# A third form tile, later stores of the gated blocks, and one pass of taps for the last column block

## The chip, the cores and the metric

The kernel runs on one core of one Trainium2 chip. The metric is the time of one execution on the device in microseconds (us). The engines go by their profile names: PE is TensorE, DVE is VectorE, ACT is ScalarE, POOL is GpSimd, and SP is SyncE, which here only issues DMA transfers. POOL issues transfers of its own, through another queue.

## The reference

A decoder layer for 256 tokens and 2048 features, in float32. The normalised input is projected once into ten parts. Two mixers use them: attention with 16 heads over low-rank latents, and a short causal convolution. Each passes a gate and a projection, and the two are merged by sigmoid gates.

```python
h = _rmsnorm(x, pre_norm_g)
(q_a, c_kv, k_rope, z_mla, c_in, b_gate, c_gate, z_conv,
 g_mla, g_conv) = jnp.split(h @ w_in, cuts, axis=-1)
q = _rmsnorm(q_a, q_a_norm_g) @ w_q_b        # 16 heads of 128 + 64 (rotary)
kv = _rmsnorm(c_kv, kv_a_norm_g) @ w_kv_b    # 16 heads of 128 + 128
attn = _causal_mla_attention(q_nope, q_rope, k_nope, k_rope, v)
y_mla = (attn * jax.nn.silu(z_mla)) @ w_o_mla
u = c_gate * c_in
u_pad = jnp.pad(u, ((0, 0), (CONV_K - 1, 0), (0, 0)))
conv = sum(conv_w[k] * u_pad[:, k:k + s] for k in range(CONV_K))   # CONV_K = 3
y_conv = (b_gate * conv * jax.nn.silu(z_conv)) @ w_o_conv
merged = jax.nn.sigmoid(g_mla) * y_mla + jax.nn.sigmoid(g_conv) * y_conv
x = x + _rmsnorm(merged @ w_out, post_norm_g)
```

## The kernel before

**Splitting.** Every float32 operand of a matmul is split into a rounded part and a rest. ACT copies the rounded part (`whi`), DVE subtracts it to get the rest (`wlo`), and PE adds three products: hi by hi, hi by lo, lo by hi. Weights come in units of 128 x 2048 numbers (1 MB) into three `raw` buffers. SP loads a unit once the DVE instruction that made the rest of the unit three before it is done. Four k-blocks of weights against both token tiles are 24 matmuls of width 512, called a unit here.

**Stage one: latents.** The products for `qa`, `ckv` and `kr`, and the tables `cos_t`, `sin_t` of the rotation.

**Stage two: the loop over 16 heads** (line 996). Each head h makes, beside its attention, one quarter of the work on a column block of 512 convolution channels: `channels(h, i)` for i = 0 to 3 is one weight unit each, and head 4j + n makes c_gate, c_in, b_gate, z_conv (n = 0 to 3) of block j. The banks `cv` are evacuated by ACT or DVE (lines 811 to 820) before the next head needs them. Between the units stand scores, softmax, `turn` and `values` of neighbouring heads. Two side jobs are cut into steps by generators:

- `make_forms` (line 871) prepares seven sums of quarters of the normalised input for the Winograd products of stage three: "11", "22", "12", "5", "6", "7" and "3", in four chunks, so 28 pieces. One step is taken at three places in each of the heads 0 to 13. In a step, `part` (line 900) takes a tile `form` from a ring of two, ACT writes its hi half (line 902), DVE its lo half (line 904 or 906). SP is told to store it to `far_form` (line 909) in the step after. Four small tiles, `u, w, f7, f3`, hold sums (line 897).
- `taps(j, t)` (line 831) makes the convolution of block j and token tile t. It brings two copies of u shifted by one and two tokens through POOL transfers into `mv1`, `mv2` and two weight rows into `cw`; in a second step it multiplies and adds them and fetches the third weight row; in a third step it finishes in `cv_f` (all products at line 853). Each token tile is a run of its own; for block 3, tile 1 is begun at the end of head 13 and tile 0 in head 14, and tile 0 ends in head 15. `channels_join` then multiplies the gate in and stores the block, turned, through POOL to `far_cv`.

**Stage three: the square products.** A list `seq` of units, in four sets (s0 to s3, "set one" to "set four" here), interleaves two kinds. `branch_block` units multiply the mixers' outputs by w_o (banks `sq`). `paired` units make two gate blocks at a time by a Winograd scheme over the forms (banks `sX`, `sZ`, `sY`; tiles `b`), with some sums made by adding POOL transfers (line 1256). When a gate tile `sa` to `sd` and its product meet, set one and two call `weigh` (line 1216): multiply, and store to `kept` one unit later on SP (line 1148). Set three and four call `merge` (line 1230): multiply, add the block fetched again into a tile `y` (POOL, line 1151), transpose on DVE (line 358), and store to `far_m` one unit later by four SP transfers (line 366). `later(n, fn)` puts fn off by n units. A store that is issued on SP waits there for its tile, and whatever is behind it in SP's queue waits too. `turned_unit` (line 964) reloads `far_at`, `far_cv` and `far_m` for the next products.

**Stage four: out.** 16 weight units against the four merged blocks `m_both`; blocks 0 and 1 are needed at once, block 2 at the fifth unit, block 3 at the seventh. Then the last norm.

The order of PE is the program's. On ACT and DVE a scheduler sets it from its estimates, but for the instructions marked by `keep_in_program_order`; the orders of SP and POOL are the program's too.

Of the kernel before, what the change touches and what calls it, by code (L numbers as in the profile page):

```python
# [82 lines left out]
def tile_layer(ctx: ExitStack, tc: tile.TileContext, xw, w0, xb, x, pos, pvec, post_g, wc, wz, wcv, wkr, wqk, wqr, wv, cwr, wsq, xf, out):  # L83
# [211 lines left out]
    cos_t = const.tile([P, S], F32, name="cos_t")  # L295
    sin_t = const.tile([P, S], F32, name="sin_t")
# [34 lines left out]
    ckv = lp.tile([P, KR, 2 * S], F32R, name="ckv")  # L331
    kr = bp.tile([P, 2, S], F32R, name="kr")
# [498 lines left out]
    def taps(j, t):  # L831

        u, parts = cv_t[:, j, t, :], []

        def bring(dst, src):

            tc.keep_in_program_order(nc.gpsimd.dma_start(out=dst, in_=src))

        for d in (1, 2):
            m = temp(f"mv{d}", (P, 512), bufs=1, tag=f"mv{d}x")  # L840
            if t:
                bring(m[:d, :], cv_t[P - d :, j, 0, :])
            else:
                tc.keep_in_program_order(nc.gpsimd.memset(m[:d, :], 0.0))
            bring(m[d:, :], u[: P - d, :])
            parts.append(m[:, :])
        def tap(d):
            cw = temp("cw", (P, 512), bufs=2)
            bring(cw[:, :], cwr[2 - d : 3 - d, 512 * j : 512 * (j + 1)].to_broadcast([P, 512]))
            return cw  # L850

        def join(dst, a, b, op):
            tc.keep_in_program_order(nc.vector.tensor_tensor(dst, a, b, op=op))
# [17 lines left out]
    def make_forms():  # L871
# [3 lines left out]
        sums_4 = [early_pool.tile([P, kq, P], F32, name=f"form_sum{i}") for i in range(4)]  # L875
        for c in range(KH // kq):
# [17 lines left out]
            u, w, f7, f3 = (f[:, :, :] for f in sums_4)  # L894
# [4 lines left out]
            def part(n, src, sign=1.0):  # L899
                f = early_pool.tile([P, kq, 2, P], F32R, name=f"form{n}_{c}", tag="form", bufs=2)  # L900
                hi, lo = f[:, :, 0, :], f[:, :, 1, :]
                nc.scalar.activation(hi, src, AF.Copy, scale=sign)
                if sign == 1.0:
                    nc.vector.tensor_tensor(lo, src, hi.bitcast(F32), op=ALU.subtract)
# [11 lines left out]
                ("5", u, 1.0, (w, u, a11, ALU.add)), ("6", w, -1.0, (f7, a11, a21, ALU.subtract)),  # L916
                ("7", f7, 1.0, (f3, w, a12, ALU.subtract)), ("3", f3, 1.0, None),
# [78 lines left out]
    for h in range(H):  # L996
        v, at = divmod(h, HV)

        if h == H - 2:
            estack.close()  # L1000
            lstack.close()
            fleft = main.enter_context(tc.tile_pool(name="fleft", bufs=1, reuse_waits="tile"))
# [40 lines left out]
        if v and at == 0 or h >= H - 2:  # L1043
            next(tap)
# [15 lines left out]
        if at == 2 or h == H - 1:  # L1060
            next(tap)
# [40 lines left out]
        if at == 1:  # L1102
            tap = taps(v, 1)
            next(tap)
        elif at == 3 and h + 1 < H:
            tap = taps(v, 0)
            next(tap)
# [4 lines left out]

    bstack.close()
# [110 lines left out]
    def fetch():  # L1224
        if wanted:
            c, t = wanted.pop(0)
            fetched[c, t] = wide(f"m{c}_{t}", "y", 2)
            again(("m", c, t), fetched[c, t])

    def merge(nc_, t):  # L1230
# [6 lines left out]
        go, _ = turned(m[:, :], g[:, :], 4, far_m[c][:, 512 * t : 512 * (t + 1)], nc.sync)  # L1237
        later(1, go)
# [144 lines left out]
    for u, m in ((s3["V7"][1], 0), (v[3][3], 1)):  # L1383
        also(u, m_load[m][0][0])
# [3 lines left out]
    def first_fetches(order):  # L1388
        wanted.extend(order)
        fetch()  # L1390
        fetch()
# [68 lines left out]

    last_m = m_load[2][0]
# [200 lines left out]
```

## Time and profile before

| | us |
|---|---|
| median of 3 runs | 1057.33 |
| the runs | 1054.04, 1057.33, 1061.59 |
| the profiled execution | 1061.88 |
| its span, first to last instruction | 1059.6 |

| engine | busy us | share of the span |
|---|---|---|
| PE | 1019.5 | 96% |
| DVE | 803.5 | 76% |
| ACT | 591.8 | 56% |
| POOL | 167.8 | 16% |

The times of the profile run from the start of the span. The heads last until about 613, the square products until 965, and out until the end. A line number in the profile is that of the instruction, often inside a helper (line 88 for every matmul), so the tile names tell more. "PE sq <- ACT whi" reads: PE sat idle before a matmul into a bank `sq`, and what ended the wait was ACT finishing a `whi`. A letter q behind an engine's name is its queue: an instruction that issues a transfer.

### The profile page before, as it was taken

How to read it: one execution, taken by the hardware profiler on the slowest of the kernel's cores; microseconds unless marked ns; L12 is line 12 of the kernel's file. 1: busy time of each engine (PE TensorE's matmuls, PEld its weight loads, DVE VectorE, ACT ScalarE, POOL GpSimd, SP SyncE). 2: the span in 40 equal slices, each digit the busy share in tenths (PEclk: the TensorE clock that was granted, in tenths of full speed). 3: DMA queues.
4: the chain of work that ended last, by engine and by line, in shares of the span. 5: the costliest groups of instructions: out<-in, count | busy, mean ns of one | idle time of the engine just before them, and what ended most of it. 6: DMA issues, size and time to landing. Idle time of an engine off the chain costs nothing.

```text
span 1059.6 us, 13048 instructions
## 1 busy us (share of the span) xinstructions
PE 1019.5 (96%) x4552; PEld 840.8 (79%) x4552; DVE 803.5 (76%) x1101; ACT 591.8 (56%) x854; POOL 167.8 (16%) x304
## 2 busy tenths in 40 slices
PE   9999999999999989999999987999998999899997
PEld 8887888887788878788888865888787788688886
DVE  7588878677797768766887696788787889586662
ACT  7666656555565555455564554564664664573551
POOL 4620421213211132112232220000000000100000
PEclk9999999999999999989999998999999999999999
DMA  9775877668775786847787899689679487956942
GB/s 368 272 236 225 288 245 262 219 205 286 228 279 203 211 271 240 293 168 240 235 298 282 307 319 373 262 302 261 236 255 355 159 292 187 284 210 242 366 186 79
DMA packets 58993, 271.02 MB, mean 256 GB/s; under 512 B 9104, under 2 KB 15888, under 8 KB 33584
## 3 DMA queue, kind: packets, MB, share of 16 engines
q1 hardware_dynamic: 45792, 226.94, 59.0%
q0 software_dynamic: 12848, 42.07, 15.0%
q10 hardware_dynamic: 288, 1.20, 0.3%
q8 instruction: 35, 0.57, 0.2%
q14 instruction: 30, 0.25, 0.1%
HBM read 241.88 MB, written 24.12 MB: 251 GB/s over the span
## 4 chain that ended last, share of the span: by engine, by line
PE 77%; DMA 11%; DVE 6%; ACT 3%; issue 1%; SPq 1%; DVEq 0%; ACTq 0%
PE cv L88 26%; PE sq L88 13%; PE out L88 8%; PE sX L88 7%; PE z L88 7%; DMA far_form<-form 6%; DMA raw<-wsq_dram 4%; PE sZ L88 3%; DVE wlo L266 2%; PE qa L88 2%; PE ckv L88 2%; PE sY L88 2%; ACT whi L265 2%; PE qn L88 1%; DMA x_area<-xf_dram 1%
## 5 line engine op out<-in xcount | busy, mean ns | idle before, releaser
L265 ACT ACTIVATE whi<-raw 128x1024 fp32r<-128x1024 f32 (+1 forms) x302 | 305.2, 1027 | 252.2 <-PE cv L88 86.1
L266 DVE TENSOR_TENSOR wlo<-raw,whi 128x1024 fp32r<-128x1024 f32 (+1 forms) x300 | 352.2, 1187 | 121.1 <-ACT whi L265 101.6
L88 PE MATMUL cv<-whi,x_both 128*128 128x512 f32 x1024 | 323.4, 392 | 8.1 <-ACT cv_f L811 4.9
L88 PEld LDWEIGHTS cv<-whi,x_both 128*128 128x128 f32 x1024 | 193.6, 189 | 50.6 <-ACT cv_f L811 6.2
L88 PE MATMUL cv<-wlo,x_both 128*128 128x512 f32 x512 | 200.6, 392 | 1.5 <-DVE wlo L266 1.5
L88 PEld LDWEIGHTS cv<-wlo,x_both 128*128 128x128 f32 x512 | 96.9, 189 | 21.2 <-DVE wlo L266 1.8
L266 DVE TENSOR_TENSOR slo_V<-b,shi_V 128x1024 fp32r<-128x1024 f32 x60 | 71.6, 1220 | 18.4 <-PE sq L88 11.7
L265 ACT ACTIVATE shi_V<-b 128x1024 fp32r<-128x1024 f32 x60 | 61.2, 1052 | 37.8 <-PE sq L88 26.9
L88 PE MATMUL z<-whi,x_both 128*128 128x512 f32 x256 | 79.9, 389 | 0.0
L88 PE MATMUL sq<-whi,cv_both 128*128 128x512 f32 x256 | 63.9, 404 | 7.7 <-ACT whi L265 7.7
L366 POOL DMA_DIRECT2D far<-via x64 | 35.4, 559 | 224.0 <-DVE via L358 222.5
L88 PE MATMUL sq<-whi,at_both 128*128 128x512 f32 x256 | 62.3, 396 | 7.8 <-ACT whi L265 7.8
L88 PEld LDWEIGHTS sq<-whi,cv_both 128*128 128x128 f32 x256 | 50.0, 197 | 19.3 <-ACT whi L265 8.7
L88 PEld LDWEIGHTS sq<-whi,at_both 128*128 128x128 f32 x256 | 48.9, 192 | 19.1 <-ACT whi L265 8.8
L88 PEld LDWEIGHTS z<-whi,x_both 128*128 128x128 f32 x256 | 48.1, 188 | 9.9
L88 PE MATMUL sX<-shi_V,form 128*128 128x512 f32 x192 | 47.8, 391 | 2.3 <-ACT sb L1300 2.3
L88 PE MATMUL z<-wlo,x_both 128*128 128x512 f32 x128 | 49.8, 389 | 0.0
L88 PE MATMUL out<-whi,m_both 128*128 128x512 f32 x208 | 49.4, 389 | 0.0
L88 PEld LDWEIGHTS out<-whi,m_both 128*128 128x128 f32 x208 | 39.0, 188 | 8.1
L88 PEld LDWEIGHTS sX<-shi_V,form 128*128 128x128 f32 x192 | 35.8, 188 | 10.9 <-ACT sb L1300 3.6
L1256 POOL DMA_DIRECT2D b<-wsq_dram x10 | 8.7, 894 | 186.1 <-ACT whi L265 125.1
L266 DVE TENSOR_TENSOR slo_Q<-b,shi_Q 128x1024 fp32r<-128x1024 f32 x28 | 33.4, 1220 | 4.7 <-PE sq L88 3.2
(301 smaller groups left out, 1560.4 us busy)
## 6 DMA issues: line engine op xcount, KB each, us to landing
raw<-wcv_dram SPq DMA_DIRECT2D x64, 1024.0 KB, 6.1
raw<-wsq_dram SPq DMA_DIRECT2D x48, 1024.0 KB, 6.8
b<-wsq_dram SPq DMA_DIRECT2D x26, 1024.0 KB, 5.2
raw<-wz_dram SPq DMA_DIRECT2D x16, 1024.0 KB, 4.8
b<-wsq_dram POOLq DMA_DIRECT2D x10, 1024.0 KB, 10.7
raw<-wqk_dram SPq DMA_DIRECT2D x8, 1024.0 KB, 7.7
far_form<-form SPq DMA_DIRECT2D x28, 256.0 KB, 7.7
form<-far_form SPq DMA_DIRECT2D x7, 1024.0 KB, 11.2
```

The lines of the kernel that those rows point to most:

```text
L88: return tc.keep_in_program_order(nc.tensor.matmul(*a, **kw))
L265: a = nc.scalar.activation(hi, src, AF.Copy)
L266: b = nc.vector.tensor_tensor(lo, src, hi.bitcast(F32), op=ALU.subtract)
L366: tc.keep_in_program_order(queue.dma_start(out=f[i], in_=m))
L1256: tc.keep_in_program_order(nc.gpsimd.dma_start(out=dst[:, :], in_=wsq[n, c + b, k], accum_op=ALU.add))
```

## The change

1. The ring of `form` tiles has three members. The sums f7 and f3 are kept in the tiles u and w, once these have been read; two of the four sum tiles fall away. `cos_t` and `sin_t` move from one pool to another.
2. `taps` takes a list of token tiles. Blocks 0 to 2 call it as before, for one tile at a time. For block 3 one run makes both token tiles: begun at the start of head 14, multiplied after the second unit of head 14, finished after the first unit of head 15. It needs a second pair of shifted copies, in a pool of its own, `mvp`. The three weight rows are fetched once and not twice.
3. `weigh` stores to `kept` four units later and not one. `merge` stores blocks 0 and 1 to `far_m` four units later, through SP as before. Blocks 2 and 3 are stored through POOL, behind all of `seq`, and the reload of block 2 is issued there too. The ring `y` has three members, and the first fetches are three.

PE's instructions are the same, in the same order. The first place where the order moves is SP's queue in set three; `turned_cv` is the reload of the convolution's blocks 2 and 3, and a `raw` or `b` row is a 1 MB weight load. Before:

```order
L1148 DMA kept_m_1_6955<-sd_6918 128x512
L1251 DMA b_1_1_6957<-wsq_dram 128x2048
L167 DMA raw_6980<-wsq_dram 128x2048
L1148 DMA kept_m_0_7057<-sa_6482 128x512
L1148 DMA kept_m_0_7059<-sb_6711 128x512
L1148 DMA kept_m_1_7061<-sc_6757 128x512
L964 DMA turned_cv_7063<-far_cv_646 128x1024
L964 DMA turned_cv_7063<-far_cv_647 128x1024
L167 DMA raw_7088<-wsq_dram 128x2048
L1251 DMA b_1_2_7090<-wsq_dram 128x2048
L1251 DMA b_1_3_7097<-wsq_dram 128x2048
L167 DMA raw_7133<-wsq_dram 128x2048
```

And now, on the same queue at the same place:

```order
L1258 DMA b_1_1_6951<-wsq_dram 128x2048
L167 DMA raw_6974<-wsq_dram 128x2048
L1155 DMA kept_m_1_7029<-sd_6914 128x512
L969 DMA turned_cv_7053<-far_cv_646 128x1024
L969 DMA turned_cv_7053<-far_cv_647 128x1024
L167 DMA raw_7078<-wsq_dram 128x2048
L1258 DMA b_1_2_7080<-wsq_dram 128x2048
L1258 DMA b_1_3_7087<-wsq_dram 128x2048
L1155 DMA kept_m_0_7123<-sa_6476 128x512
L1155 DMA kept_m_0_7125<-sb_6707 128x512
L1155 DMA kept_m_1_7127<-sc_6753 128x512
L167 DMA raw_7129<-wsq_dram 128x2048
```

The stores of sa, sb and sc have moved from ahead of the reload to behind three loads; the store of sd stands behind two more loads. On DVE and ACT the scheduler now puts the splits of that reload (`cv_both`) ahead of some of the weights' splits.

The second place is SP's queue in set four, from the load of `b_1_1` on. Before:

```order
L1251 DMA b_1_1_7601<-wsq_dram 128x2048
L167 DMA raw_7624<-wsq_dram 128x2048
L1251 DMA b_1_2_7626<-wsq_dram 128x2048
L1251 DMA b_1_3_7649<-wsq_dram 128x2048
L366 DMA far_m_648<-sa_7086 32x4x128 x4
L366 DMA far_m_649<-sb_7344 32x4x128 x4
L366 DMA far_m_649<-sc_7394 32x4x128 x4
L167 DMA raw_7728<-wsq_dram 128x2048
L167 DMA raw_7752<-wsq_dram 128x2048
```

And now:

```order
L1258 DMA b_1_1_7595<-wsq_dram 128x2048
L167 DMA raw_7618<-wsq_dram 128x2048
L1258 DMA b_1_2_7620<-wsq_dram 128x2048
L1258 DMA b_1_3_7643<-wsq_dram 128x2048
L366 DMA far_m_648<-sd_7554 32x4x128 x4
L167 DMA raw_7712<-wsq_dram 128x2048
L167 DMA raw_7736<-wsq_dram 128x2048
L366 DMA far_m_648<-sa_7076 32x4x128 x4
L366 DMA far_m_649<-sb_7340 32x4x128 x4
L366 DMA far_m_649<-sc_7392 32x4x128 x4
```

Two weight loads have moved ahead of the stores of sa, sb and sc, and the store of sd behind four loads.

The third place is DVE's queue at the end of the heads, from the softmax of head 15 (`via`) to its `values` (`f<-o`). `mv` and `cv_f` rows at line 853, now 843, are the products of the taps. Before, from the third split behind `via` on:

```order
L266 TENSOR_TENSOR wlo_1024_5614<-raw_5568,whi_1024_5613 128x1024
L266 TENSOR_TENSOR wlo_0_5647<-raw_5607,whi_0_5646 128x1024
L266 TENSOR_TENSOR pt<-p,pt 128x384
L853 TENSOR_TENSOR mv_5509<-mv_5509,cw 128x512
L853 TENSOR_TENSOR mv_5512<-mv_5512,cw 128x512
L266 TENSOR_TENSOR wlo_1024_5651<-raw_5607,whi_1024_5650 128x1024
L853 TENSOR_TENSOR mv_5509<-mv_5509,mv_5512 128x512
L853 TENSOR_TENSOR cv_f<-cv_f,cw 128x512
L853 TENSOR_TENSOR cv_f<-cv_f,mv_5509 128x512
L434 TENSOR_TENSOR f<-o_5679,half 128x256
```

And now:

```order
L266 TENSOR_TENSOR wlo_1024_5611<-raw_5566,whi_1024_5610 128x1024
L843 TENSOR_TENSOR cv_f<-cv_f,cw 128x512
L266 TENSOR_TENSOR wlo_0_5642<-raw_5604,whi_0_5641 128x1024
L843 TENSOR_TENSOR cv_f<-cv_f,mv_5311 128x512
L843 TENSOR_TENSOR cv_f<-cv_f,cw 128x512
L266 TENSOR_TENSOR pt<-p,pt 128x384
L843 TENSOR_TENSOR cv_f<-cv_f,mv_5317 128x512
L266 TENSOR_TENSOR wlo_1024_5646<-raw_5604,whi_1024_5645 128x1024
L434 TENSOR_TENSOR f<-o_5674,half 128x256
```

The three `mv` products of tile 0 have moved up, to just behind `via`, and the two last products of tile 1 have moved down to stand here. On POOL the third weight row now comes behind the eight `far<-via` stores of heads 14 and 15, and the two reloads of p behind that.

```diff
@@ pools
-    cos_t = const.tile([P, S], F32, name="cos_t")
-    sin_t = const.tile([P, S], F32, name="sin_t")
...
+    cos_t = bp.tile([P, S], F32, name="cos_t")
+    sin_t = bp.tile([P, S], F32, name="sin_t")
@@ taps
-    def taps(j, t):
+    def taps(j, ts, tiles=None):
...
+        both = []
+        for i, t in enumerate(ts):
+            u, parts = cv_t[:, j, t, :], []
+            for d in (1, 2):
+                m = tiles and tiles[i]
+                m = m[d - 1] if m else temp(f"mv{d}", (P, 512), bufs=1, tag=f"mv{d}x")
+                if t:
+                    bring(m[:d, :], cv_t[P - d :, j, 0, :])
+                else:
+                    tc.keep_in_program_order(nc.gpsimd.memset(m[:d, :], 0.0))
+                bring(m[d:, :], u[: P - d, :])
+                parts.append(m[:, :])
+            both.append((u, parts))
         cws = [tap(d) for d in (1, 2)]
         yield
-        for a, cw in zip(parts, cws):
-            join(a, a, cw[:, :], ALU.mult)
-        join(parts[0], parts[0], parts[1], ALU.add)
+        for u, parts in both:
+            for a, cw in zip(parts, cws):
+                join(a, a, cw[:, :], ALU.mult)
+            join(parts[0], parts[0], parts[1], ALU.add)
         cw = tap(0)
         yield
-        join(u, u, cw[:, :], ALU.mult)
-        join(u, u, parts[0], ALU.add)
+        for u, parts in both:
+            join(u, u, cw[:, :], ALU.mult)
+            join(u, u, parts[0], ALU.add)
         yield
@@ make_forms
-        sums_4 = [early_pool.tile([P, kq, P], F32, name=f"form_sum{i}") for i in range(4)]
+        sums_2 = [early_pool.tile([P, kq, P], F32, name=f"form_sum{i}") for i in range(2)]
...
-                f = early_pool.tile([P, kq, 2, P], F32R, name=f"form{n}_{c}", tag="form", bufs=2)
+                f = early_pool.tile([P, kq, 2, P], F32R, name=f"form{n}_{c}", tag="form", bufs=3)
...
-                ("5", u, 1.0, (w, u, a11, ALU.add)), ("6", w, -1.0, (f7, a11, a21, ALU.subtract)),
-                ("7", f7, 1.0, (f3, w, a12, ALU.subtract)), ("3", f3, 1.0, None),
+                ("5", u, 1.0, (w, u, a11, ALU.add)), ("6", w, -1.0, (u, a11, a21, ALU.subtract)),
+                ("7", u, 1.0, (w, w, a12, ALU.subtract)), ("3", w, 1.0, None),
@@ the loop over heads
+            mvp = mstack.enter_context(tc.tile_pool(name="mvp", bufs=1))
+            tap = taps(3, (1, 0), [[mvp.tile([P, 512], F32, name=f"mv_{d}") for d in (1, 2)], None])
+            next(tap)
...
-        if v and at == 0 or h >= H - 2:
+        if v and at == 0 or h == H - 1:
             next(tap)
...
-        if at == 2 or h == H - 1:
+        if at == 2:
             next(tap)
...
-        elif h == H - 2:
-            tap = taps(3, 0)
-            next(tap)
...
-        if at == 1:
-            tap = taps(v, 1)
+        if at == 1 and h < H - 3:
+            tap = taps(v, (1,))
             next(tap)
@@ weigh, fetch, merge
-        later(1, lambda: keep(("m", c, t), g))
+        later(4, lambda: keep(("m", c, t), g))
...
-            fetched[c, t] = wide(f"m{c}_{t}", "y", 2)
+            fetched[c, t] = wide(f"m{c}_{t}", "y", 3)
...
-        go, _ = turned(m[:, :], g[:, :], 4, far_m[c][:, 512 * t : 512 * (t + 1)], nc.sync)
-        later(1, go)
+        go, _ = turned(m[:, :], g[:, :], 4, far_m[c][:, 512 * t : 512 * (t + 1)], nc.gpsimd if c > 1 else nc.sync)
+        later(0 if c > 1 else 4, go)
         later(1, fetch)
@@ the plan of stage three
-    for u, m in ((s3["V7"][1], 0), (v[3][3], 1)):
-        also(u, m_load[m][0][0])
+    also(s3["V7"][1], m_load[0][0][0])
...
-        fetch()
-        fetch()
+        for _ in range(min(3, len(order))):
+            fetch()
...
+    m_load[1][0][0]()
     last_m = m_load[2][0]
```

More of the change, by code (lines that the diff above doesn't have):

```diff
@@ L829, in channels_join @@
         return lambda: None
-    def taps(j, t):
-        u, parts = cv_t[:, j, t, :], []
+    def taps(j, ts, tiles=None):
         def bring(dst, src):
             tc.keep_in_program_order(nc.gpsimd.dma_start(out=dst, in_=src))
[L839 to L846, printed above, removed]
         def tap(d):
@@ L893, in make_forms @@
             a12, a22 = area[:, 1, :, :P], area[:, 1, :, P:]
-            u, w, f7, f3 = (f[:, :, :] for f in sums_4)
+            u, w = (f[:, :, :] for f in sums_2)
             def tt(o, a, b, op):
@@ L1001, in tile_layer @@
             lstack.close()
+            mstack = ctx.enter_context(ExitStack())
             fleft = main.enter_context(tc.tile_pool(name="fleft", bufs=1, reuse_waits="tile"))
@@ L1101, in tile_layer @@
             coming.append(channels_join(v, 1))
-        if at == 1:
-            tap = taps(v, 1)
+        if at == 1 and h < H - 3:
+            tap = taps(v, (1,))
             next(tap)
         elif at == 3 and h + 1 < H:
-            tap = taps(v, 0)
+            tap = taps(v, (0,))
             next(tap)
@@ L1110, in tile_layer @@
         arrive()
+    mstack.close()
     bstack.close()
```

## The prediction

> **What bounds the kernel now.** I read the page first, for the busy shares.
>
> ```profile
> PE 1019.5 (96%) x4552; PEld 840.8 (79%) x4552; DVE 803.5 (76%) x1101; ACT 591.8 (56%) x854; POOL 167.8 (16%) x304
> ```
>
> TensorE is the bound, and the change leaves its instructions as they are, in number and in order. What can be won is the time in which TensorE stands still or runs slowly. So the second view was the list of waits. Its columns are the total in us, the number and the longest.
>
> ```profile
> PE sq L88 <- ACT whi L265: 15.5, 4, 6.2
> PE cv L88 <- ACT cv_f L811: 4.9, 3, 1.8
> PE cv L88 <- ACT cv_w L815: 3.1, 1, 3.1
> PE sc L88 <- DVE kn L266: 2.6, 3, 1.7
> PE sq L88 <- DVE wlo L266: 3.0, 3, 1.9
> ACT form L902 <- DMA far_form<-form: 40.8, 15, 5.7
> ```
>
> The first five are 29.1 us of TensorE. The second to fourth lie in the loop over heads, the first and fifth in the square products (sq, sX, sZ, sY). The last row is ScalarE's: 15 of the 28 form pieces wait until the piece two before them is stored. The third view, the chain of waits in order of time (start, length, what), ties the two together and prices the slow running.
>
> ```profile
> 238.42 11.06 DMA far_form<-form
> 249.83 0.68 ACT cv_f L811
> 451.22 16.61 PE cv L88 x60
> 634.17 13.34 DMA raw<-wsq_dram
> 648.73 7.09 PE sq L88 x24
> 796.51 20.26 DMA raw<-wsq_dram
> 817.99 7.37 PE sq L88 x24
> 899.92 6.79 DMA raw<-wsq_dram
> 907.93 7.17 PE sq L88 x24
> 965.13 87.06 PE out L88 x384
> ```
>
> The last row is 16 units of 24 matmuls of full width, 5.44 us each when nothing hinders them. The 60 after 451.22 should take 13.60 and take 16.61: 3.0 lost behind a wait of 3.1. The 24 at 648.73, 817.99 and 907.93 lose another 1.65, 1.93 and 1.73. The waits ahead of the last two are the 3.35 and 4.35 here:
>
> ```profile
> 817.99 0.50 PE L88 MATMUL sq<-whi,cv_both 128*128 128x512 f32 x1 [3.35 <-ACT whi L265]
> 907.93 0.80 PE L88 MATMUL sq<-whi,cv_both 128*128 128x512 f32 x1 [4.35 <-ACT whi L265]
> ```
>
>  The reason for the slow stretches is the granted clock (last three columns: clock, DMA share, GB/s):
>
> ```profile
> 450.00:455.00 5.00, 3.78 (x9) 3.02 (x10) 4.15 (x11) 3.32 (x7) 0.00 (x0) 0.52 0.34 134
> ```
>
> The Trainium skill, page "TensorE: Matmul & The Clock Gate", section "What's actually happening", says that the clock halves after at least one idle window of about 3.4 us. By that rule a wait of 3.1 costs itself alone, and the sum below would be 3.0 smaller. The trace disagrees, and I go by its row.
>
> **Part one: the third form tile.** A form piece is copied by ScalarE, finished by VectorE, and stored by SP one step later. With two tiles, piece k+2 waits for the store of k; with three, piece k+3 does. ScalarE takes its work in order, so an evacuation (cv_f, cv_w) or a half of a split behind a waiting piece waits too.
>
> ```profile
> 249.51 0.42 ACT L902 ACTIVATE form<-form_sum 128x256 fp32r<-128x256 f32 x1 [5.75 <-DMA far_form<-form]
> 360.27 0.42 ACT L902 ACTIVATE form<-x_area 128x256 fp32r<-128x256 f32 x1 [2.33 <-DMA far_form<-form]
> 361.82 0.42 ACT L902 ACTIVATE form<-form_sum 128x256 fp32r<-128x256 f32 x1
> ```
>
> The extra tile gives each piece one more step of the column products, 5.44 us or more, against a longest wait of 5.75. The tightest kind of place is 361.82: with three tiles this piece needs the store that released its neighbour at 360.27, and has 1.5 us to spare. So all 15 waits should go. With them go the three waits for cv_f (4.9), the one for cv_w (3.1) with its slow stretch (3.0), and the longest for kn (1.7), whose split stood behind a piece: 4.9 + 3.1 + 3.0 + 1.7 = **12.7**. What is late next is nothing that I can see: the waits removed on ScalarE are longer than those of TensorE behind them. Bounds: 9.7 if the slow stretch stays for another reason, 13.6 if all of kn goes. Keeping f7 and f3 in the tiles u and w adds a write after a read on VectorE, one step later and off the path: nothing. The tables' and sums' new places move no instruction.
>
> **Part two: the taps of block 3.** Ten products stay ten. Before, VectorE reached the last five while their weights were still under way:
>
> ```profile
> 599.64 0.69 DVE L853 TENSOR_TENSOR mv<-mv,cw 128x512 f32<-128x512 f32 x1 [6.61 <-DMA cw<-cwr_dram]
> 601.52 1.22 DVE L266 TENSOR_TENSOR wlo<-raw,whi 128x1024 fp32r<-128x1024 f32 x1
> 605.32 0.42 DVE L434 TENSOR_TENSOR f<-o,half 128x256 f32<-128x256 f32 x1
> 601.69 0.39 ACT L433 ACTIVATE half<-o 128x256 f32<-128x256 f32 x1 [6.31 <-PE o L88]
> ```
>
> Behind that wait of 6.61 stood a wlo, which frees a raw buffer for SP, and then f, ready for VectorE at 601.69 + 0.39 = 602.08 and done from 605.32. From there VectorE has work without a break until the load at 634.17 is let go, and that load ends the wait of 6.2. So the whole stretch moves by 605.32 - 602.08 = 3.2. I take **3.0**, and not the sum of the waits (15.5 - 4.35 - 3.35 = 7.8 for whi, 3.0 for wlo), since the shorter ones only feed the last. Bounds: 8 (6.6 of the wait and a slow stretch of 1.65) if the loads freed earlier also land earlier; -2 (an estimate) if the reloads of p arrive late: on POOL the last weights of the taps now wait for six products, behind them queue both reloads of p, for those ScalarE's copy pt waits, and for that TensorE's o. Two copies and two memsets come a head earlier, under that head's products, and three of six weight loads fall away.
>
> **Part three: stores four units late.** SP issues in order; a store that waits for VectorE holds every load behind it. In set three (start, length, queue):
>
> ```profile
> 787.45 0.33 SPq L1148 DMA_DIRECT2D kept_m<-sa  x1
> 790.19 1.93 SPq L964 DMA_DIRECT2D turned_cv<-far_cv  x2
> 785.00:790.00 5.00, 5.00 (x24) 4.13 (x22) 5.00 (x6) 3.38 (x4) 0.87 (x1) 1.00 0.43 79
> 810.00:815.00 5.00, 4.64 (x21) 3.52 (x19) 3.84 (x3) 0.00 (x0) 0.00 (x0) 1.00 1.01 424
> ```
>
> The two halves of turned_cv (1.05 MB together) now go ahead of sa, into a stretch where the DMA engines are 0.43 busy, and not into the full queue ahead of the load at 796.51. At 424 GB/s that is 2.5 us off the 20.26. The load itself is issued when VectorE has freed its buffer, and VectorE now takes four splits of cv_both before that; this costs no more than the queue hides. Of the wait of 3.35, 0.9 would be left, and I count on no slow stretch (1.93) behind so short a one. Between nothing and 5.3 I take **3.0**; below, -2, if the later issue shows.
>
> Set four is clearer:
>
> ```profile
> 886.15 1.78 SPq L366 DMA_DIRECT2D far_m<-sa  x4
> 896.95 2.86 SPq L366 DMA_DIRECT2D far_m<-sc  x4
> 883.15 2.35 DVE L266 TENSOR_TENSOR wlo<-raw,whi 128x1024 fp32r<-128x1024 f32 x2
> 880.00:885.00 5.00, 5.00 (x24) 4.14 (x23) 5.00 (x5) 2.91 (x4) 0.00 (x0) 1.00 0.03 11
> ```
>
> SP sat before sa and again before sc, with the load of 899.92 behind both. That load's buffer is free once the first wlo at 883.15 is done, and it now stands ahead of sa, with the engines idle (0.03). Issued at 884.4 and 6.79 under way, it lands by 892; TensorE wants it at 907.93 - 4.35 = 903.6. That wait and its slow stretch of 1.73 go: **6.1**; 3 if the adding transfers on POOL crowd it. The stored blocks are read again a set later, so storing them late keeps nobody waiting; the third buffer y lets a third fetch leave earlier: nothing on the path.
>
> **Tail.** The stores of the last two merged blocks move from SP to POOL, their reloads behind them.
>
> ```profile
> L366 SPq DMA_DIRECT2D far_m<-sc x8: 302/448/950, 896.9 to 973.7; - x8
> DMA to landing us min/median/max: 1.9/4.6/7.3
> DMA to landing us min/median/max: 5.1/8.8/9.2
> ```
>
> (The second row is that of the via stores, which POOL issues already, the third that of turned_m.) Behind these stores POOL holds only their own reloads. Issued to 973.7 + 4 x 0.1, the reload of block 2 starts near 975, lands at 984, and is split by 986. TensorE wants it after four of the sixteen units of 87.06: 965.13 + 21.8 = 986.9. Nothing, then, by 1 us; with 7.3 and 9.2 it would cost up to 2 (an estimate).
>
> Sum: 12.7 + 3.0 + 3.0 + 6.1 = 24.8. The profiled execution took 1061.9 (span 1059.6), 4.6 above the median of 1057.3 and at the upper end of the runs. It would become 1037.1. If its excess of 4.6 lies in waits that the change removes, the median comes to the same; if not, to 1032.5. I forecast **1034**.
>
> **Rivals.** *Another wait takes their place in the heads.* VectorE stays 76% busy or more, and the two shorter kn waits, 0.9 together, would be the next kind. Half of 12.7 kept: 1034 + 6.3 = 1040. Against it: ScalarE, at 56%, has room. Chance 0.16.
>
> *The DMA engines are the bound of the square part.* At 1.01 and 424 GB/s, order does not help; part two and set three give nothing, the rest stays: 1034 + 6 = 1040, with half of set four gone too 1043. For it: 20.26 for a load that takes 6.79 elsewhere. Chance 0.15.
>
> *The last blocks come late over POOL's queue.* Were landings to double in traffic (4.6 and 8.8 more), TensorE would wait 12.5 at 986.9 and run slowly for 1.7: 1048. The Trainium skill, page "DMA: Bandwidth & Descriptors", section "Issuing engine by pattern", gives simple stores to Sync and calls its hardware path generally faster. Chance 0.05.
>
> *The forms only wait elsewhere,* for stores that still follow raw loads on SP: parts one and two give nothing, 1034 + 15.7 = 1050. Against it: the spare time at 361.82. Chance 0.09.
>
> *Slower: the pieces themselves get in front of what TensorE waits for.*
>
> ```profile
> L904 DVE TENSOR_TENSOR form<-form_sum,form 128x256 fp32r<-128x256 f32 x12 | 5.0, 420 | 15.1 <-ACT form L902 14.9
> ```
>
> Unheld, 28 pieces of 0.42 on ScalarE and 0.42 on VectorE, with a sum of like size for most, now stand in new places of both queues. If each cost its 1.26 on TensorE's path, 35 us would outweigh 24.8: 1057.3 + 10.5 = 1068. It decides from 24.8 / 28 = 0.9 a piece. Against it: pieces that waited for nothing, such as that at 361.82, have no TensorE wait behind them. Chance 0.04.
>
> **How the numbers follow.** The forecast has 0.51; its own range, from the bounds (9.7 to 13.6, -2 to 8, -2 to 5.3, 3 to 6.1, tail -2 to 0, all ends seldom together), is 1025 to 1043. To leave out no more than the last rivals, the range goes to 1048. Within 1% (10.6 us, about what this kernel's runs can tell from no change) means 1047 to 1068. Faster: 0.51 + 0.16 + 0.15 + part of the third: 0.85. Slower: 0.03. The rest: 0.12.
>
> **What would show it.** In the list of waits, ScalarE's row for far_form gone, and with it cv_f and cv_w; a clock of 1.00 around 450; no wait of VectorE for cw near 600, the wait before the fourth sq unit still there but 3 us sooner; turned_cv issued before 780 and the set-three wait under 2; no wait in set four; out still 87.06 for 384. I am wrong if ScalarE's form waits remain, if the load that ended at 816.8 still lands as late against TensorE, or if out takes over 89.

## The result, and the profile after

The changed kernel took 1045.54 us (median of 4 runs, 1044.07 to 1049.55) against 1057.67 before on the same chip (1054.04 to 1061.59): a ratio of 0.988, 95% interval 0.984 to 0.992. That is 12.1 us, half of the 24.8 that the sum gave. The time lies 11.5 above the forecast of 1034: inside the stated range (to 1048), but above the 1043 at which the prediction's own bounds end. The profiled execution took 1049.55 with a span of 1047.8, 11.8 less than before.

For every trace I made the same sum: over all 4551 intervals between the starts of successive matmuls, what each took beyond the usual interval of its kind (0.227 us for a width of 512). This is the time that TensorE loses, by waiting or by a slow clock, and it can be split by stage. Heads is all up to the first matmul into `sq`, the transition the wait that this matmul ends (1.8 us before the change, none in any other trace) and the 55 us behind it, set three the stretch from 170 to 235 us behind it, set four from 265 to 315.

| lost, us | heads | transition | set three | set four | out | all |
|---|---|---|---|---|---|---|
| before | 23.1 | 15.4 | 7.3 | 7.1 | 1.7 | 55.3 |
| changed | 16.5 | 14.8 | 8.6 | 1.0 | 1.7 | 43.4 |
| won | 6.6 | 0.6 | -1.4 | 6.1 | 0 | 11.9 |
| forecast | 12.7 | 3.0 | 3.0 | 6.1 | 0 | 24.8 |

The last column agrees with the spans (11.8) and with the medians (12.1). So one of the four gains came as forecast, and three did not. First the busy shares and the list of waits after the change (total us, number, longest):

```profile
PE 1016.8 (97%) x4552; PEld 839.4 (80%) x4552; DVE 802.4 (77%) x1101; ACT 591.4 (56%) x854; POOL 174.4 (17%) x317
...
PE sq L88 <- ACT whi L265: 9.1, 2, 5.7
PE cv L88 <- ACT cv_f L811: 5.0, 2, 3.7
PE sq L88 <- DVE wlo L266: 5.0, 5, 1.8
PE sc L88 <- DVE kn L266: 1.9, 2, 1.3
ACT form L907 <- DMA far_form<-form: 36.8, 14, 7.6
```

ScalarE's waits for the form stores, which should all have gone, are almost all there: 14 of 36.8 us, against 15 of 40.8. The wait for `cv_f` is as long in total as before, in two pieces and not three. The chain of waits (start, length, what) shows the same pattern as before at three of its places and none at the fourth:

```profile
375.96 10.75 DMA far_form<-form
387.06 0.68 ACT cv_f L811
387.78 4.63 PE cv L88 x10
...
625.24 13.81 DMA raw<-wsq_dram
640.26 8.40 PE sq L88 x24
...
792.05 18.84 DMA raw<-wsq_dram
812.11 7.36 PE sq L88 x24
...
892.34 10.88 PE sq L88 x48
...
953.24 87.05 PE out L88 x384
```

At 387 a store ends, a form copy starts, the evacuation `cv_f` behind it ends, and TensorE goes on after 3.7 us. At 640 and 812 the two weight loads are still what TensorE waits for, for 5.69 and 3.37. In set four two units run 10.88 without a break where 4.35 was waited, and `out` takes what it took.

SP's queue ahead of the load of 792.05 (start, time of issue, what; the last row merges four loads, the first of which leaves at 792.05):

```profile
773.03 0.80 SPq L969 DMA_DIRECT2D turned_cv<-far_cv  x2
...
788.67 0.98 SPq L1258 DMA_DIRECT2D b<-wsq_dram  x2
789.70 0.88 SPq L1155 DMA_DIRECT2D kept_m<-sa  x1
790.62 0.77 SPq L1155 DMA_DIRECT2D kept_m<-sb  x1
791.43 0.51 SPq L1155 DMA_DIRECT2D kept_m<-sc  x1
792.05 22.75 SPq L167 DMA_DIRECT2D raw<-wsq_dram  x4
```

The reload `turned_cv` has gone ahead, to 773.03, as forecast. But the stores of sa, sb and sc now come right ahead of the load that TensorE waits for.

### The profile page after: what moved, and what is told of

Read it like the earlier page. It is cut to its first block, busy times and chain, and to the rows that moved or that the text cites. A ratio compares the mean times of both kernels' runs of the same rounds, so it can differ in the third digit from the quotient of the medians.

```text
span 1047.8 us, 13032 instructions
## 1 busy us (share of the span) xinstructions
PE 1016.8 (97%) x4552; PEld 839.4 (80%) x4552; DVE 802.4 (77%) x1101; ACT 591.4 (56%) x854; POOL 174.4 (17%) x317
## 4 chain that ended last, share of the span: by engine, by line
PE 82%; DMA 9%; DVE 4%; ACT 3%; issue 1%; SPq 1%; DVEq 0%; ACTq 0%
PE cv L88 28%; PE sq L88 15%; PE out L88 8%; PE z L88 8%; PE sX L88 7%; DMA far_form<-form 4%; PE sZ L88 3%; DMA raw<-wsq_dram 3%; PE qa L88 2%; PE sY L88 2%; PE ckv L88 2%; PE qn L88 1%; DVE wlo L266 1%; PE kn L88 1%; ACT whi L265 1%
```

## The experiments

All runs stand beside runs of the kernel before on the same chip, and a ratio is to those; its interval is 0.003 to 0.004 to either side, some 3 to 4 us. Three chips were used, on which the kernel before had medians of 1062.1 (two form tiles, three in place, old taps, `kept` six late), 1057.4 (once more, form reloads later, `far_m` one late, in place + six) and 1059.6 (the other four). So across these groups ratios can be compared and medians cannot. What is smaller than that is read from the loss of TensorE, by stage, as above. (The expectations left out of the heads' loss each stretch of 10 us that lost under 0.3; so 21.7 and 15.0 there are 23.1 and 16.5 in the tables.)

| lost, us | heads | transition | set three | set four | all | median, us | ratio |
|---|---|---|---|---|---|---|---|
| changed, once more | 15.4 | 13.0 | 8.4 | 1.0 | 40.3 | 1047.7 | 0.990 |
| two form tiles | 19.9 | 13.6 | 8.6 | 1.0 | 45.6 | 1050.7 | 0.989 |
| three, copy in place | 9.8 | 12.5 | 8.7 | 1.0 | 34.4 | 1040.4 | 0.981 |
| two, copy in place | 12.6 | 12.9 | 8.8 | 1.0 | 37.8 | 1043.8 | 0.985 |
| old taps | 11.7 | 13.6 | 8.4 | 1.0 | 37.2 | 1044.7 | 0.985 |
| form reloads later | 22.8 | 9.9 | 8.9 | 1.0 | 45.1 | 1046.2 | 0.989 |
| `kept` six late | 13.9 | 14.2 | 2.6 | 1.0 | 34.1 | 1042.2 | 0.982 |
| `kept` one late | 19.0 | 13.9 | 8.3 | 1.0 | 44.6 | 1048.0 | 0.989 |
| `far_m` one late | 18.0 | 12.1 | 8.4 | 1.0 | 41.9 | 1049.0 | 0.991 |
| two y tiles | 13.5 | 13.4 | 8.0 | 1.0 | 38.9 | 1046.6 | 0.987 |
| in place + six | 11.9 | 12.3 | 2.7 | 1.0 | 30.4 | 1036.9 | 0.979 |
| in place + six + later | 9.0 | 10.2 | 2.6 | 1.0 | 25.3 | 1032.6 | 0.975 |

### How much of a trace repeats

The changed kernel, as it is.

> The changed kernel itself once more, to stand beside the experiments on one chip, and to see which of its TensorE waits are the same in a second trace. Theory (the waits of the square part are set by order and traffic, those of the heads by how near a store lands to the piece that waits for it): the waits before the fourth sq unit (6.1 lost) and in set three (3.5 lost) come again within 1 us, while the wait at 387.78 (3.8 lost) does not, since two kernels with the same heads lost 1.4 to 1.7 there. Rival (all waits repeat): 3.8 again. Time 1045.5 either way, within the spread of its runs (1044 to 1050).

The two waits of the square part came again, 5.66 and 3.52 lost against 6.10 and 3.54. Of the heads' waits the one near 387 lost 2.2 and not 3.8, and one near 251 lost 2.5 and not 1.5. As expected, then. Eight of these traces have three form tiles in the scheduler's places, and the same order on ScalarE and VectorE up to 560 us. Their heads lost between 11.7 and 22.8, 16.3 in the mean. A change in the heads is not read from one such trace.

### The form ring

The ring put back to two, all else as changed:

```diff
-                f = early_pool.tile([P, kq, 2, P], F32R, name=f"form{n}_{c}", tag="form", bufs=3)
+                f = early_pool.tile([P, kq, 2, P], F32R, name=f"form{n}_{c}", tag="form", bufs=2)
```

> The changed kernel with the ring of form tiles back at two, all else as changed. Theory (the third tile was spent on an earlier place in ScalarE's queue, and only what was in the way at the end of each chunk was won): the heads lose what they lost before the change, 21.7 us of TensorE against 15.0 now, so the time is 1045.5 + 6.7 = 1052, and ScalarE's row of waits for far_form is back at 15 waits of about 41 us (now 14 waits of 36.8). Rival (the heads' gain is not from the ring): 1045.5, with TensorE's losses in the heads still near 15.

```profile
ACT form L907 <- DMA far_form<-form: 40.5, 15, 6.1
```

The waits are back at 15 of 40.5, and the heads lost 19.9: 3.6 more than the mean of the eight with three tiles, and inside their spread. The kernel before, the other trace with two tiles, lost 23.1, or 6.8 more. So the ring is worth 3.6 to 6.8 by these two traces, about half of what was forecast. That it won this much is likely and not shown: the ratio, 0.989, does not differ from the 0.988 and 0.990 with three tiles.

The reason is in ScalarE's order. Here is ScalarE before the change, and then after it, in the same head (last: idle time before, and what ended it):

```profile
232.80 0.42 ACT L902 ACTIVATE form<-x_area 128x256 fp32r<-128x256 f32 x1
...
261.44 0.42 ACT L902 ACTIVATE form<-form_sum 128x256 fp32r<-128x256 f32 x1 [3.99 <-DMA far_form<-form]
```

```profile
231.99 0.42 ACT L907 ACTIVATE form<-form_sum 128x256 fp32r<-128x256 f32 x1 [0.18 <-DMA far_form<-form]
...
248.13 0.42 ACT L907 ACTIVATE form<-form_sum 128x256 fp32r<-128x256 f32 x1 [5.28 <-DMA far_form<-form]
248.45 0.67 ACT L811 ACTIVATE cv_f<-cv,r_both 128x512 f32<-128x512 f32 x1
...
260.29 0.42 ACT L907 ACTIVATE form<-form_sum 128x256 fp32r<-128x256 f32 x1 [4.21 <-DMA far_form<-form]
```

The places and the waits are the same, but each holds the next piece: at 232.80 the third piece of the chunk stood (from `x_area`), and at 231.99 stands the fourth (from `form_sum`). The scheduler has put the pieces one place ahead: from the third of each chunk on, 17 of 20 stand exactly where the piece before them stood, and the other three within four instructions of it. The orders listed with the change begin in set three; this one, which moves from 89 us on, is not among them. A piece now takes the tile of three pieces before instead of two, and meets its store just as much in flight: 5.28 where 5.75 was waited (the row at 249.51), 4.21 for 3.99.

So the next edit keeps the third tile and takes the scheduler's choice away:

```diff
-                nc.scalar.activation(hi, src, AF.Copy, scale=sign)
+                tc.keep_in_program_order(nc.scalar.activation(hi, src, AF.Copy, scale=sign))
```

> The changed kernel with three form tiles, but ScalarE's copy into the tile kept at its place in the program, so that the scheduler cannot move it ahead. Theory (the scheduler moved every piece one place ahead, so a piece still meets the store three before it just in flight): ScalarE's row for far_form falls from 14 waits of 36.8 us to under 5 waits of 10, and TensorE's waits at 249.18 and 387.78 (1.5 and 3.8) go with the slow stretch behind the second (about 1.5): 1045.5 - 6.8 = 1039. Rival (the stores are late because of SP's queue or the DMA engines): the waits stay, 1045. Second rival (a later piece makes its own store wait in SP's queue, with the weight loads behind it): 1050.

No wait for a form store is left. The program's place is a later one than the scheduler chose even with two tiles: the third piece of this chunk, at 232.80 before the change, stands eight instructions further back. ScalarE in the same head, and then TensorE's two longest waits in all the heads:

```profile
246.98 0.40 ACT L907 ACTIVATE form<-x_area 128x256 fp32r<-128x256 f32 x1
248.15 0.69 ACT L811 ACTIVATE cv_f<-cv,r_both 128x512 f32<-128x512 f32 x1
```

```profile
PE cv L88 <- ACT cv_w L815: 1.9, 1, 1.9
PE sc L88 <- DVE kn L266: 0.8, 1, 0.8
```

The heads lost 9.8, and 11.9 and 9.0 in the two later kernels with this edit: 11 to 14 less than before the change, and 8 to 11 less than with two tiles in the scheduler's places. That is about the 12.7 forecast for the ring, and it came from the place of the copy. The time agrees: a ratio of 0.981 (0.978 to 0.985) against the 0.990 (0.986 to 0.994) of the changed kernel. The third tile itself can then be tested:

```diff
-                f = early_pool.tile([P, kq, 2, P], F32R, name=f"form{n}_{c}", tag="form", bufs=3)
-                nc.scalar.activation(hi, src, AF.Copy, scale=sign)
+                f = early_pool.tile([P, kq, 2, P], F32R, name=f"form{n}_{c}", tag="form", bufs=2)
+                tc.keep_in_program_order(nc.scalar.activation(hi, src, AF.Copy, scale=sign))
```

> The changed kernel with two form tiles and ScalarE's copy kept at its place in the program. With three tiles and this place, all but four of the 28 copies started after the store two before them had landed; the four were 0.3, 0.7 and 3.2 us ahead of it, or 0.3 behind. Theory (the place made the waits, not the number of tiles): at most 5 waits of 6 us in all for far_form, TensorE's loss in the heads near 8 to 10 as with three tiles kept in place, and 1041. Rival (the third tile is needed): 10 waits or more, a loss of 15 or more in the heads, 1047.

```profile
ACT form L907 <- DMA far_form<-form: 1.3, 2, 0.9
...
PE sc L88 <- DVE kn L266: 3.4, 1, 3.4
```

With two tiles in place, two waits of 1.3 us together are left. The heads lost 12.6, somewhat over the 8 to 10 expected, with one wait of 3.4 for `kn` in it. Whether that wait belongs to the ring or to the spread, one trace does not tell. The place made most of the waits, not the number of tiles.

### The taps of block 3

The taps as before the change, all else as changed:

```diff
-            tap = taps(3, (1, 0), [[mvp.tile(...) for d in (1, 2)], None])   # head 14, begun
-            next(tap)
...
+        elif h == H - 2:
+            tap = taps(3, (0,))
+            next(tap)
...
-        if at == 1 and h < H - 3:
+        if at == 1:
             tap = taps(v, (1,))
```

> The changed kernel with the taps of the last column block made as before, one run for each token tile. Theory (the new taps let the weight load of the fourth sq unit go sooner by about 2 us against the heads, but TensorE then ran slowly for longer behind the wait): the time is 1045.5 + 0.5 = 1046, VectorE waits about 6.6 for cw again, and the wait before the fourth sq unit is about 6 to 8 long. Rival (the taps gave their 3.0 and another change in that stretch took it away): 1048.5.

The transition lost 13.6, in the middle of the 12.1 to 14.8 of the traces with the new taps and the old form reloads. VectorE's rows at the end of the heads, with the old taps:

```profile
584.65 0.69 DVE L843 TENSOR_TENSOR mv<-mv,cw 128x512 f32<-128x512 f32 x1 [3.03 <-DMA cw<-cwr_dram]
586.34 0.69 DVE L843 TENSOR_TENSOR mv<-mv,cw 128x512 f32<-128x512 f32 x1 [1.00 <-DMA cw<-cwr_dram]
590.70 0.42 DVE L434 TENSOR_TENSOR f<-o,half 128x256 f32<-128x256 f32 x1
...
590.28 0.39 ACT L433 ACTIVATE half<-o 128x256 f32<-128x256 f32 x1 [6.31 <-PE o L88]
```

The wait of 6.61 is 3.03 and 1.00 here, and `f` starts at 590.70, right when ScalarE's half is done (590.28 + 0.39 = 590.67). VectorE's order in this stretch is, row for row, that of before. So the order by itself does not cost the 3.2 us that the prediction counted. Why the weights `cw` came later in the trace of before, by that execution or by another part of the change, one trace of each does not show. The load of the fourth `sq` unit was let go 30.1 us behind the start of that half with the old taps and 30.1 with the new (32.5 before the change). The ratio, 0.985, is no worse than that of the changed kernel, and its heads lost less (11.7). The rival (3.0) falls. Of the theory the outcome stands, that the new taps bring nothing here beyond the spread of some 1.5, but not its reason: the new taps did not let the load go sooner.

### The transition

The form blocks are reloaded five units ahead of their use:

```diff
-        loads.append((need - 1, need - AHEAD, lambda n=n: bring_form(n)))
+        loads.append((need - 1, need - 5, lambda n=n: bring_form(n)))
```

> The changed kernel with the form blocks for set one reloaded five units ahead of their use and not eight, so that the weight load of the fourth sq unit (625.24, 13.81 under way) is issued ahead of the reload at 622.28 and the next ones come behind more weight loads. Theory (the stretch is crowded, but order within it matters): two reloads of 1.05 MB no longer share the engines with the load; at the 270 GB/s of 625:630 one of them is 3.9 us, so the wait of 5.7 falls under 2 and the slow stretch of 3 behind it goes: 1045.5 - 6 = 1039.5. Rival (the DMA engines are the bound there: 610 to 650 at a share of 1.0, so what is moved back is late for the next unit): the loss only moves to sX or a later sq, 1045.

SP of the changed kernel, and then of this one:

```profile
622.28 0.33 SPq L937 DMA_DIRECT2D form<-far_form  x1
625.24 0.33 SPq L167 DMA_DIRECT2D raw<-wsq_dram  x1
```

```profile
631.55 0.33 SPq L167 DMA_DIRECT2D raw<-wsq_dram  x1
632.10 0.33 SPq L937 DMA_DIRECT2D form<-far_form  x1
...
631.55 9.99 DMA raw<-wsq_dram
```

The load was 9.99 under way and not 13.81, TensorE's wait fell to 2.84 where under 2 was expected (5.26 in the second trace of the changed kernel), and the transition lost 9.9, 3 less than the 13.0 there. No later unit waited for a form block. So order counts there, by about half of what I gave it, and the rival (bound by the engines whatever the order) falls. The time does not show it: this execution lost 22.8 in the heads, the most of the eight.

### Set three

First the stores of sets one and two six units late, then one:

```diff
-        later(4, lambda: keep(("m", c, t), g))
+        later(6, lambda: keep(("m", c, t), g))
```

> The changed kernel with the blocks of sets one and two stored six units late instead of four, which in set three puts the stores of sa, sb and sc (0.75 MB) behind the weight load issued at 792.05 (18.84 us under way) and not ahead of it. Theory (order within a full DMA queue decides, and moving the reload of the convolution ahead was undone by these stores and a third fetch taking its place): the load lands 0.75 MB / 424 GB/s = 1.8 us sooner, the wait of 3.4 at 812.11 falls to 1.6, and the slow stretch of 1.9 behind it goes: 1045.5 - 3.7 = 1042. Rival (POOL's adding transfers and the other loads keep the DMA engines full whatever the order): the wait stays above 3, 1045.5.

```profile
786.25 0.33 SPq L167 DMA_DIRECT2D raw<-wsq_dram  x1
786.62 0.47 SPq L1155 DMA_DIRECT2D kept_m<-sa  x1
...
786.25 17.08 DMA raw<-wsq_dram
804.54 5.75 PE sq L88 x24
```

The load now stands ahead of sa, and TensorE's wait before that unit is 0.27 and not 3.37, with no slow stretch: set three lost 2.6 against 8.4, 5.8 less where 3.7 was expected. The load was issued 18.3 us ahead of its unit (786.25 to 804.54), and in the changed kernel 20.1 (792.05 to 812.11), of which 3.4 was TensorE's wait. The scheduler also moved things: VectorE now makes all four splits of the reload, and so frees its buffer, ahead of a sum of `b` and of the second half of a weight split, where two of the four stood behind them. How the gain divides between that and the stores I did not separate.

```diff
-        later(4, lambda: keep(("m", c, t), g))
+        later(1, lambda: keep(("m", c, t), g))
```

> The changed kernel with the blocks of sets one and two stored one unit late, as before the change, and all else as changed. Theory (in set three four units are no better than one: the reload of the convolution went ahead, but the stores of sa, sb and sc and SP's time for them took its place ahead of the load): the wait of 3.4 in set three stays within 1, 1047.7. Rival (four units won the 3.0 forecast there, and something else lost it): the wait is 6 long, 1050.7.

```profile
813.29 1.92 PE L88 MATMUL sq<-whi,cv_both 128*128 128x512 f32 x4 [4.42 <-ACT whi L265]
```

Set three lost 8.3, as with four units: one wait of 4.42 before that unit in place of one of 0.96 and one of 3.37. The theory stands. Four units late bring nothing there; one place further, six, bring 5.8.

### Set four

First the merged blocks stored one unit late again, then two y tiles again:

```diff
-        later(0 if c > 1 else 4, go)
+        later(0 if c > 1 else 1, go)
```

> The changed kernel with the merged blocks 0 and 1 stored one unit late on SP, as before the change, and all else as changed. Theory (set four's gain of 6.1 is all from these stores no longer standing ahead of two weight loads): the wait of about 4.4 in front of the sq unit after the fourth Winograd pair of set four is back with its slow stretch, 1045.5 + 6 = 1051.5. Rival (the place of set four in time, or the third y tile, took the wait away): no wait there, 1045.5.

The rival came true: no wait in set four, 1.0 lost as in the changed kernel. What had held SP before shows on POOL, before the change and then in this kernel:

```profile
864.45 0.55 POOL L1151 DMA_DIRECT2D m<-kept_m  x1 [68.86 <-DVE sd L358]
886.41 0.55 POOL L1151 DMA_DIRECT2D m<-kept_m  x1 [21.42 <-DVE sa L358]
```

```profile
856.96 0.55 POOL L1158 DMA_DIRECT2D m<-kept_m  x1 [68.24 <-DVE sd L358]
```

With two y tiles the fourth fetch had to wait until sa was transposed, and only then could sc be merged, transposed and stored: at 896.95, with the load of 899.92 behind it. With a third tile that fetch is gone by 857, sc is stored from 886.54, and the two loads behind it leave at 888.39 and 888.88, early enough.

```diff
-            fetched[c, t] = wide(f"m{c}_{t}", "y", 3)
+            fetched[c, t] = wide(f"m{c}_{t}", "y", 2)
...
-        for _ in range(min(3, len(order))):
+        for _ in range(min(2, len(order))):
             fetch()
```

> The changed kernel with two y tiles and two first fetches, as before the change, and the stores still four units late. Before the change the store that held SP in set four (sc at 896.95) waited for a merge whose fetch POOL had issued only at 886.41; with a third y tile that fetch leaves at 858.64. Theory (late stores and the third y tile each suffice): no TensorE wait for whi in set four, and in set three 0.26 MB less in the crowd, 0.6 us at 424 GB/s: 1047.7 - 0.6 = 1047. Rival (the third y tile alone did it, as the run with stores one unit late suggests): the wait of 4.4 with its slow stretch is back, 1047.7 + 6 = 1053.7.

Again no wait in set four, although the fourth fetch is late again, 22 us behind the third. So the late stores and the third tile each do without the other, and the change did it twice. No run has both put back with all else as changed, so it is not shown that nothing else in the change would have removed the wait. In set three the fetch that no longer stands in the crowd is worth 0.4 (8.0 against 8.4), near the 0.6 expected.

### Together

Copy in place, and `kept` six units late:

```diff
+                tc.keep_in_program_order(nc.scalar.activation(hi, src, AF.Copy, scale=sign))
...
+        later(6, lambda: keep(("m", c, t), g))
```

> The changed kernel with the form copies kept at their program's place and the blocks of sets one and two stored six units late, together. Theory (the two stand in different stages, heads and set three, and add up): TensorE loses 34.4 us with the first alone, of which 6.5 in set three between 790 and 810, and about 6 of them go: 28.5 lost and a time of 1040.4 - 6 = 1034.5. Rival (an earlier set three meets the same traffic again): 1040.

The loss is 30.4 and the median 1036.9, each about 2 worse than expected, all of it in the heads (11.9 for 9.8). Set three is down by 6.0, as expected. They add up.

The form reloads later as well:

```diff
+        loads.append((need - 1, need - 5, lambda n=n: bring_form(n)))
```

> Three edits on the changed kernel together: form copies kept in place, blocks of sets one and two stored six units late, form blocks reloaded five units ahead. Theory (they stand in three different stages and add up): the loss between 600 and 650, 12.3 with the first two, falls by the 3.1 that the third alone won there (13.1 to 10.0): 1036.9 - 3.1 = 1033.8. Rival (with the rest moved the stretch is bound by what the DMA engines carry): 1036.9.

The transition lost 10.2, the heads 9.0, and the median is 1032.6 (1031.5 to 1035.1), a ratio of 0.975 to the kernel before, with an interval of 0.971 to 0.979. The busy shares and TensorE's longest waits in the square part and the heads:

```profile
PE 1010.9 (98%) x4552; PEld 836.8 (81%) x4552; DVE 801.9 (78%) x1101; ACT 590.8 (57%) x854; POOL 174.1 (17%) x317
...
PE sq L88 <- ACT whi L265: 3.3, 2, 3.1
...
PE cv L88 <- ACT cv_w L815: 1.6, 1, 1.6
```

This kernel is faster than the one before and the changed one: TensorE's loss is down from 55.3 to 25.3, and 10.2 of what is left lie in the transition.

## Why the prediction was half right

- **The time.** The sum was 12.9 too high (6.1 in part one, 2.4 in part two, 4.4 in set three). The 1045.5 fell into the range because its upper end had been moved from 1043, where the bounds of the terms ended, to 1048 for the sake of the rivals. That is partly luck. Two of the prediction's own signs of being wrong came true: ScalarE's form waits remain, and the set-three load lands as late against TensorE as before (a wait of 3.37 for 3.35).
- **Part one, 12.7 forecast, 6.6 measured in the first pair of traces, 3.6 to 6.8 by the runs.** The step that failed is that the extra tile gives each piece one more step of the column products, so that all 15 waits should go. It took each piece to stay at its place in ScalarE's queue. The scheduler moved the pieces one place ahead, and 14 waits of 36.8 remained. The size given to those waits, some 12.7 of TensorE, is borne out: with the copy kept in place the heads lost 11 to 14 less than before (8 to 11 less than the second trace with two tiles). The clock was 1.00 around 450 in that trace as forecast, but not for my reason, since in two others with the same form ring TensorE waited 3.4 for `cv_w` there again. Of the rivals, "the forms only wait elsewhere" had the mechanism, though it put it down to SP, and "another wait takes their place" had the size, 1040 with half the gain kept.
- **Part two, 3.0 forecast, 0.6 measured in the first pair of traces.** VectorE no longer waits for `cw` near 600, as forecast. The mis-sized term is the 3.2 us taken from `f` at 605.32: it was read from one execution, and the same order lost nothing in the run with the old taps, whose transition (13.6) lies among those with the new (12.1 to 14.8). That the wait before the fourth `sq` unit would remain was right.
- **Part three, set three, 3.0 forecast, -1.4 measured.** The reload went ahead of 780, as forecast, where the DMA engines had room (a share of 0.74 and 0.98 from 770 to 780, with the reload in it). What failed is the count: it took 1.05 MB out of the queue ahead of the load and left out that the stores themselves, 0.79 MB, and a third fetch came to stand there instead. SP's time for them counts too: two loads of `b` and three stores took it from 788.67 to 792.05. The lower bound of -2, "if the later issue shows", held.
- **Part three, set four, 6.1 forecast, 6.1 measured.** The loads went ahead of the stores and no wait was left. But "the third buffer y: nothing on the path" was wrong: with the stores of blocks 0 and 1 put back to one unit late, no wait came back. I read that SP sat before sc, and did not ask what sc had waited for.
- **Tail, 0 forecast, 0 measured:** 87.05 for the 384 matmuls.
- **The base.** The profiled execution lay 4.6 above its median before, and 4.0 after, so that the sum of one trace and the medians agree (11.8 and 12.1).
- **The rival of the DMA engines** is refuted in its strict form: with another order, 3 us went in the transition and 5.8 in set three.

## What to carry to other kernels

A deeper ring buys time only if its users stay where they are: where a scheduler sets the order, compare the orders row by row, and keep the producer in place if it has moved ahead. A transfer that is moved later stands ahead of something else, so list what it now delays, SP's time to issue it included. And before a stage's gain is put down to one edit, follow the released wait back to its first cause, and take two traces, since single waits of 2 to 4 us came and went here under the same order.

## What the runs showed of the hardware

**A wait of 1.8 us can already halve the clock.** In the heads, over the 14 traces, none of 15 single waits between 1.35 and 1.77 us had a slow stretch behind it (the excess in the next 9 us was under 0.3). Of 10 waits between 1.81 and 2.36, 5 had one, of 1.4 to 1.7 us lost. Of 8 from 2.54 to 3.66, 7 had one, of 1.6 to 3.0; one of 3.45 had none. The shortest that had one, 1.82 us at 305.6 in the run with copies in place and `kept` six late, was followed by a clock of 0.50 from 307 to 309. The rows of two windows of the changed kernel (engines' busy time, last the clock, DMA share and GB/s) show such a stretch behind the wait of 3.66, and none around 450 in that trace:

```profile
390.00:395.00 5.00, 5.00 (x16) 3.92 (x15) 4.88 (x9) 1.67 (x5) 2.18 (x4) 0.66 0.87 206
450.00:455.00 5.00, 5.00 (x24) 4.14 (x23) 5.00 (x13) 3.28 (x9) 0.00 (x0) 1.00 0.57 192
```

The Trainium skill, page "TensorE: Matmul & The Clock Gate", section "What's actually happening", names one idle window of about 3.4 us, and says that the window runs free. A window that runs free fits the chance in the middle group; a limit of 3.4 does not fit waits half as long.

**Full DMA engines did not always move the same.** In the transition the busy share was 1.0 throughout, but the rate was not:

```profile
625.00:630.00 5.00, 4.01 (x18) 3.00 (x16) 5.00 (x4) 0.56 (x2) 0.00 (x0) 1.00 1.00 270
635.00:640.00 5.00, 0.00 (x0) 0.00 (x0) 0.00 (x0) 0.85 (x1) 0.00 (x0) 0.50 1.00 419
...
618.10 0.95 POOL L1263 DMA_DIRECT2D first_rb<-wsq_dram  x1 [0.24 <-issue]
...
first_rb<-wsq_dram POOLq DMA_DIRECT2D x2, 1024.0 KB, 13.6
```

From 620 to 630 the rate was 265 to 270 GB/s, from 635 to 650 it was 419 to 433. In the first stretch POOL's two loads that add to their target were under way (issued at 618.10 and 620.65, 13.6 to landing). That these made the difference was not tried by itself.
